# Weight sums of the up-projection made during the mixers' projection, a third activation fetched early in the down stage, the delayed norm's fetches pinned

## The chip, the cores and the metric

The kernel runs on one core of a Trainium2 chip. The metric is the device time of one execution in microseconds; the figure for a kernel is the median of its runs. All numbers below are microseconds (us) unless marked ns. The engines are PE (TensorE, matmuls), PEld (its weight loads), DVE (VectorE), ACT (ScalarE), POOL (GpSimd) and SP (SyncE, which here only issues DMAs). L12 is line 12 of the kernel before, unless a line of the changed kernel is named as such.

## The reference

One layer of a trunk is computed for 2048 prompt rows and 8 x 16 sample rows of width 1024, all in float32:

```
h = RMSNorm(x);  z = h @ w_in                      (1024 -> 3592)
A = chunk-band attention(z);  B = mLSTM(z)
x = x + RMSNorm(concat(A, B) @ w_out)              (1024 -> 1024)
u = RMSNorm(x) @ w_up                              (1024 -> 2 x 2816)
y = causal depthwise convolution of width 3 over u, plus bias
x = x + RMSNorm((gelu(y_gate) * y_up) @ w_down)    (2816 -> 1024)
```

The outputs are x, the new key and value caches, the mLSTM states and the last two rows of u for the next convolution.

## The kernel before

**Precision.** Every float32 operand of a matmul is split into a high part (a cast on ACT, L1250) and a low part (raw minus high, a subtraction on DVE, L1251), and each product is three matmuls (`mm3`, L93 to L97). So each block of weights costs a load, a cast and a subtraction before PE can use it.

**The mixers' projection** (L1186 to L1241) runs in two halves of the rows, and in each half over 14 groups of columns of w_in (`GROUPS`, L1140). A group's weights are loaded in two pieces of 512 KB by `load_group` (L1144 to L1165, tile wi_raw, issue at L1155, cast at L1161, subtraction at L1162) while the group before is on PE. The work of a group is cut into units; after each unit the loop steps the weights of the next group, the norms of the next half's rows (`norm_steps`), and `pump` (L171), which mixes in pieces of attention and mLSTM according to their costs on PE and DVE. Almost all loads of this stage stand in the one queue of SP, in order: weights (wi_raw), keys and values (kraw, qraw, vraw, and the caches skr, svr), masks and biases, states. A load whose buffer is still in use holds what stands behind it. The row of a norm's gains is read by `norm_row` (L87) into a tile with the tag "grow", of which there is one buffer. Then `project` (L956) multiplies with w_out, adds the residual on POOL (L1021) and stores it.

**The FFN** runs in three blocks of rows (6, 6 and 5 tiles of 128 rows). Each block has an up stage and a down stage.

*Up stage* (L1462 to L1501). For each of the 22 f (128 gate columns and 128 up columns) the two 128-column products of the two halves of the block are made with seven block products in place of eight, in the manner of Strassen and Winograd; each is 12 matmuls, so 84 per f. Four of the seven weight blocks are sums of blocks of w_up. The quarters of a raw [128, 2048] slice w_up[f] are called a11, a12, a22, a21. In block 0, `load_quads` (L1255) loads the four raw quarters, makes four sums on POOL (L1267, 128x512 each) and stores them to a DRAM scratch `wsd` (L1269); blocks 1 and 2 load three raw quarters and four sums from `wsd` (L1278). `load_up` (L1282) splits the seven quarters. `ahead_of` calls it two half steps ahead. Behind the products come the corrections on DVE (L1475, L1477, L1490, L1403), the convolution `conv` (copies of a two-row halo on POOL L1414 and L1419, ACT L1422, DVE L1423 and L1424, the Gelu on ACT L1426), the product g on DVE (L1496, and L1499 for the sample rows), and its store to DRAM gd (L1501).

*Down stage* (L1507 to L1580). For each half dh of the output columns and each k of 22, g of f=k is fetched again (`fetch`, L1438 to L1447, tile gr), split (`split_g`, L1449, tiles gh and gl) and multiplied, 18 matmuls of 128x512 per k (15 in block 2). k=0 and k=1 of dh=0 are fetched in the up stage, at f=20, and split at f=21; after that `fetch(dh, k + 1)` follows the split of k. gr of k=2 stands in SP's queue behind the store of g of f=21.

*The delayed norm.* For blocks 0 and 1 the last norm of a row tile needs sums that are ready only at the end of the block. `later` (L1353 to L1365) does it in pieces, each two fetches (L1357, L1358), a product on DVE (L1360), an add on POOL (L1361) and a store (L1362). The pieces are handed out in the next block's down stage between the k.

**What sets the order.** The program is written in one order, and a scheduler (the tile context at L1675) moves each instruction on its engine by a time that it works out itself when the kernel is built; `keep_in_program_order` exempts an instruction from that. So an operation can end up far ahead of the place where it is written. Buffers also bind: tiles q (`quad`, L1041) have 11 buffers, tiles yq (`row`, L1044) three.

Of the kernel before, what the change touches and what calls it, by code (L numbers as in the profile page):

```python
# [17 lines left out]
P = 128  # L18
# [26 lines left out]
def hymba_step(ctx: ExitStack, tc: tile.TileContext, I: dict, O: dict):  # L45
# [1085 lines left out]
    def late_B():  # L1131

        for i in (P5, P2, P4, P3):
# [3 lines left out]
            nc.scalar.copy(hi, lo.bitcast(F32))  # L1137
            nc.vector.tensor_tensor(lo, lo.bitcast(F32), hi, op=ALU.subtract)  # L1138

    GROUPS = ["va0", "qk0", "qk1", "va1", "qk2", "qk3", "qb0", "vo0", "qb1", "vo1", "qb2", "vo2", "qb3", "vo3"]  # L1140
    SRC = {g: i for i, g in enumerate(["va0", "qk0", "qk1", "va1", "qk2", "qk3",
                                       "qb0", "vo0", "qb1", "vo1", "qb2", "vo2", "qb3", "vo3"])}
# [24 lines left out]
    def norm_steps(half):  # L1167

        for ci, tiles in enumerate(HALVES[half]):
            ch = phT.tile([P, 2, KT, 384], F32R, tag="hT", name=f"hT{half}_{ci}", bufs=3)  # L1170
            chunks.append(ch)
            for j, t in enumerate(tiles):
                norm_tile(t, ch, j, ps_big)
                yield 0.9, 2.5
# [3 lines left out]
    pipes += [Pipe(att_stream()), Pipe(mem_stream())]  # L1178
    chunks = []
    norms = norm_steps(0)  # L1180
    next(norms)
    pend = load_group(0)
    for _ in pend[2]:
# [2 lines left out]
    for n_, (half, gi) in enumerate(seq):  # L1186
        wh, wl, _ = pend
        split = iter([])
        if n_ + 1 < len(seq):
            pend = load_group(seq[n_ + 1][1])  # L1190
            split = pend[2]
        g = GROUPS[gi]
        i = int(g[2])
        nm = f"{g}_{half}"
        if g[:2] == "va":
            it = group_rows(wh, wl, half, chunks, vd[i], nm, 264 if gi == 0 else 256,
                            [O["v_prompt"][i], O["v_sample"][i].unsqueeze(1)])
        elif g[:2] == "qk":
            it = group_T(wh, wl, half, chunks, [qTd[i], kTd[i]], [-(DA ** -0.5), None], nm,
                         [None, [O["k_prompt"][i], O["k_sample"][i]]])  # L1200
        elif g[:2] == "qb":
            it = group_T(wh, wl, half, chunks, [[t_[:, c, :] for t_ in qkbd[i]] for c in range(2)],
                         [None, DH ** -0.5], nm)
        else:
            it = group_rows(wh, wl, half, chunks, vobd[i], nm)
        if half == 0 and gi == 13:
            chunks = []
            norms = norm_steps(1)
        if n_ == len(seq) - 1:
            out = project([0, 1, 2, 3, 4, 5, 6, 7, SAMPLE, 8, 9, 10, 11, 12, 13, 14, 15])  # L1210
            split = w_out_steps()
            next(split)
            next(out)
        for u, (pe, dve) in enumerate(it):
            ahead = []
            if n_ < len(seq) - 1 or u >= 6:
                ahead.append(next(split, (0.0, 0.0)))
            if n_ == len(seq) - 1 and u == 12:
                ahead.append(next(out))
            if (half == 0 and gi == 13 and u >= 6 and u % 2 == 0) or (gi == 0 and u % 2 == 0):  # L1220
                ahead.append(next(norms, (0.0, 0.0)))
            pump(pe + sum(a[0] for a in ahead), dve + sum(a[1] for a in ahead))
        for _ in split:
            pass
        if gi == 0:
            if half == 0:
                nc.sync.dma_start(bgate, I["b_gate"].broadcast_to([P, 8]))
                nc.sync.dma_start(gatt, I["g_att"])
                heads.append(build_bias)
                mems.append(lambda: prep(prep_sample()))  # L1230
            mems.append(lambda half=half: prep(prep_prompt(half)))
        if g[:2] == "qk":
            attention(i, half)
            if half == 0 and i == 3:
                heads.insert(len(heads) % 4, lambda: attention_sample(0, EARLY))
            if half == 1 and i == 0:
                heads.insert(len(heads) % 4, lambda: attention_sample(EARLY, DB))
        if g[:2] == "vo":
            mems.append(lambda i=i, half=half: mlstm(i, half))
            if half == 0:  # L1240
                mems.append(lambda i=i: mlstm_sample(i))  # L1241
# [8 lines left out]
        nc.scalar.copy(h, r)  # L1250
        nc.vector.tensor_tensor(l, r, h, op=ALU.subtract)  # L1251

    raws = {}

    def load_quads(b, f, g):  # L1255

        src = lambda i: I["w_up"][f][:, i * 512:(i + 1) * 512]
        if b == 0 and g == 0:
            q = []
            for i in range(4):  # L1260
                q.append(quad(f"wu{f}_{i}"))
                nc.sync.dma_start(q[i], src(i))
            a11, a12, a22, a21 = q
            s1, s2, s3, s4 = [quad(f"ws{f}_{i}") for i in range(4)]
            for o, x, y, op in ((s1, a21, a22, ALU.add), (s2, s1, a11, ALU.subtract), (s3, a11, a21, ALU.subtract),
                                (s4, a12, s2, ALU.subtract)):
                nc.gpsimd.tensor_tensor(o, x, y, op=op)  # L1267
            for i, o in enumerate((s2, s3, s1, s4)):
                nc.sync.dma_start(wsd[f][:, i * 512:(i + 1) * 512], o)  # L1269
            raws[f] = [a12, a22, s4]  # L1270
            return [a11, s2, s3, s1]
        if b == 0:
            return raws.pop(f)
        kept = lambda i: wsd[f][:, i * 512:(i + 1) * 512]
        out = []
        for i, s_ in enumerate([[src(0), kept(0), kept(1), kept(2)], [src(1), src(2), kept(3)]][g]):
            r = quad(f"wu{b}_{f}_{g}_{i}")
            nc.sync.dma_start(r, s_)  # L1278
            out.append(r)
        return out  # L1280
# [72 lines left out]
    def later(t, rs):  # L1353

        def unit(half):
            v, x, c = quad(f"f{half}{t}"), quad(f"x{half}{t}"), half * 512
            nc.sync.dma_start(v, (f0d, f1d)[half][t])  # L1357
            nc.sync.dma_start(x, x2d[t][:, c:c + 512])  # L1358
            yield 0.0, 0.0
            nc.vector.scalar_tensor_tensor(v, v, rs, g3[:, c:c + 512], op0=ALU.mult, op1=ALU.mult)  # L1360
            nc.gpsimd.tensor_tensor(v, v, x, op=ALU.add)  # L1361
            nc.sync.dma_start(out_rows(t)[:, c:c + 512], v)  # L1362
            yield 0.0, 1.0

        return [unit(half) for half in range(2)]  # L1365
# [21 lines left out]
    for b, tiles in enumerate(FBLOCKS):  # L1387
# [48 lines left out]
        n2 = nt * P // 2  # L1436

        def fetch(dh, k, early=False):  # L1438
            if k >= NF:
                return  # L1440
            if early:
                g[dh, k] = [quad(f"gr{b}_{dh}_{k}_{i}")[:, :n2] for i in range(2)]
                for i, r in enumerate(g[dh, k]):
                    nc.sync.dma_start(r, gd[b][k][:, i * n2:(i + 1) * n2])
            else:
                g[dh, k] = row(f"gr{b}_{dh}_{k}")
                nc.sync.dma_start(g[dh, k][:, :2 * n2], gd[b][k][:, :2 * n2])  # L1447
# [14 lines left out]
        for f in range(NF):  # L1462
# [20 lines left out]
            if f == NF - 1:  # L1483
                split_g(0, 0, w3_tile)
                split_g(0, 1, w3_tile)
            ug = u_tile(f"ug{nm}")
            product(P2, w[0], a, onto=True)
            nc.scalar.copy(ug[:, 2:2 + n], a[:, :n])
# [18 lines left out]
        for dh in range(2):  # L1507
# [9 lines left out]
            for c in range(6):  # L1517
# [16 lines left out]
                if tail and c >= 4:  # L1534
                    places = []
                    for i in ((0, 1) if c == 4 else (2,)):
                        t_ = p3.tile([P, 2, 4, 384], F32R, tag=f"B{i}", name=f"gtail{i}", bufs=1)
                        t_ = t_.rearrange("p a k n -> p (a k n)")
                        places += [t_[:, x * 768:(x + 1) * 768] for x in range(4)]
                    for k in ks:  # L1540
                        split_g(dh, k, lambda name: places.pop())
                        fetch(dh, k + 1)
                    if c == 4:
                        wh4, wl4 = wh, wl
                        continue
                    for j in range(nt):
                        for k in range(16, 20):
                            down(j, k, wh4, wl4)
                        for k in ks:
                            down(j, k, wh, wl)  # L1550
                        finish(b, j, load_rest(b, j), *evacuate(b, j, accs[j], 1), res[j])
                    continue
                for k in ks:
                    if (dh, k) not in parts:
                        split_g(dh, k, w3_tile)
                    if k + 1 == NF and dh == 0:
                        fetch(1, 0)
                    elif dh == 1 or k >= 1:
                        fetch(dh, k + 1)
                    for j in order if k == NF - 1 else range(nt):  # L1560
                        down(j, k, wh, wl)
                    if k >= 1:
                        ahead.step()
# [115 lines left out]
```

## Time and profile before

| what | value |
|---|---|
| median of 3 runs | 2866.95 us (2863.55 to 2875.75) |
| profiled execution, its own time | 2872.21 us |
| span of its trace | 2870.5 us |
| TensorE clock granted (mean) | 0.985 |
| up stage of block 0, of block 1 | about 1331 to 1694, 1894 to 2219 |
| last up product of block 2 | 2698 |
| loads of w_up (256 KB each) / of the sums / stores of sums | 220 / 176 / 88 |

The profile lists, for one execution, the busy time of each engine, groups of equal instructions with their mean duration and the idle time of the engine ahead of them, with what ended that idle time (the sign <-). A row of the timeline is: start, duration, engine, line, operation, output <- inputs, shapes, and in square brackets the idle time before it and its releaser. A row of the view by windows gives busy time and instruction count of each engine in a stretch, then the granted clock, the busy share of the DMA engines and GB/s.

### The profile page before, as it was taken

To read this page: it belongs to the slowest core of one execution; us is meant where nothing else is said; L and a number is where in the kernel's file an instruction comes from. 1 tells how busy PE (TensorE), PEld (TensorE's weight loads), DVE (VectorE), ACT (ScalarE), POOL (GpSimd) and SP (SyncE) were. 2 spreads that over 40 slices of the span, in tenths; PEclk is the share of its full clock that TensorE was granted. 3 is DMA by queue.
4 is the path that set the end of the run, shared out by engine and by line. 5 is a ranking of instruction groups with operands and counts; after the bars stand their busy time and mean duration, and the time that the engine had idled before them with its cause. 6 is when DMAs were issued, how large, how long until landed. Compare 5 with 4: busy or idle time off the path is not lost.

```text
span 2870.5 us, 47064 instructions
## 1 busy us (share of the span) xinstructions
PE 2752.3 (96%) x16587; PEld 2566.0 (89%) x16587; DVE 1899.5 (66%) x3345; ACT 1405.6 (49%) x2827; POOL 561.8 (20%) x964
## 2 busy tenths in 40 slices
PE   8899999999999999999999989999999899999898
PEld 7899989989899998878989978899999778999787
DVE  5344455645456678576999976467777754888755
ACT  4344555534356676343444445345554443555433
POOL 1000010211000003255555410011111210222311
PEclk9999999999999999999999999999999999999899
DMA  4544355556555564366444545645444775555766
GB/s 163 171 120 124 110 174 152 177 161 194 169 154 153 157 192 148 106 198 211 152 166 144 167 141 171 217 147 158 148 149 162 235 242 160 171 174 181 234 222 200
DMA packets 312122, 486.04 MB, mean 169 GB/s; under 512 B 55282, under 2 KB 148174, under 8 KB 311758
## 3 DMA queue, kind: packets, MB, share of 16 engines
q1 hardware_dynamic: 273294, 449.21, 50.1%
q10 hardware_dynamic: 38592, 33.83, 3.5%
q8 instruction: 130, 2.13, 0.3%
q14 instruction: 106, 0.87, 0.1%
HBM read 359.36 MB, written 126.70 MB: 169 GB/s over the span
## 4 chain that ended last, share of the span: by engine, by line
PE 49%; DVE 7%; issue 2%; DMA 2%; ACT 1%; POOL 1%; SPq 0%; DVEq 0%; ACTq 0%; POOLq 0%
PE uec L95 5%; PE uec L96 5%; PE uec L97 5%; PE dn L97 4%; PE dn L96 4%; PE dn L95 4%; PE ua L95 3%; PE ua L97 2%; PE ua L96 2%; PE dnm L95 2%; PE dnm L97 2%; PE dnm L96 2%; PE wo L97 2%; PE wo L95 2%; PE wo L96 2%
## 5 line engine op out<-in xcount | busy, mean ns | idle before, releaser
L95 PE MATMUL uec<-B,wuh 128*128 128x384 f32 (+1 forms) x720 | 236.2, 329 | 7.9 <-DVE uu L1490 7.9
L1251 DVE TENSOR_TENSOR gl<-gr,gh 128x768 fp32r<-128x768 f32 (+3 forms) x132 | 117.8, 897 | 188.2 <-ACT gh L1250 188.1
L96 PE MATMUL uec<-B,wuh 128*128 128x384 f32 (+1 forms) x720 | 235.6, 327 | 0.4 <-DVE B L1138 0.4
L97 PE MATMUL uec<-B,wul 128*128 128x384 f32 (+1 forms) x720 | 233.0, 327 | 0.0
L1250 ACT CAST gh<-gr 128x768 fp32r<-128x768 f32 (+3 forms) x132 | 101.5, 773 | 238.2 <-PE dn L96 200.0
L95 PE MATMUL dn<-wdh,gh 128*128 128x512 f32 x466 | 185.1, 397 | 7.9 <-DVE ug L1403 7.9
L96 PE MATMUL dn<-wdl,gh 128*128 128x512 f32 x466 | 185.9, 399 | 0.0
L1251 DVE TENSOR_TENSOR wul<-wu,wuh 128x512 fp32r<-128x512 f32 x255 | 179.3, 742 | 9.4 <-ACT wuh L1250 6.6
L1250 ACT CAST wuh<-wu 128x512 fp32r<-128x512 f32 x255 | 141.6, 617 | 71.3 <-PE uec L96 67.5
L97 PE MATMUL dn<-wdh,gl 128*128 128x512 f32 x466 | 170.4, 398 | 0.0
L96 PE MATMUL vo<-wi_l,hT 128*128 128x256 f32 x544 | 155.7, 286 | 0.0
L95 PE MATMUL vo<-wi_h,hT 128*128 128x256 f32 x544 | 154.9, 285 | 0.6 <-DVE mt L199 0.6
L97 PE MATMUL vo<-wi_h,hT 128*128 128x256 f32 x544 | 155.3, 285 | 0.0
L387 DVE CUSTOM_DVE_ANT_0 tmp<-s,nb 128x640 f32<-128x640 f32 (+4 forms) x128 | 94.3, 737 | 77.1 <-PE s L377 73.6
L95 PEld LDWEIGHTS uec<-B,wuh 128*128 128x128 f32 x720 | 135.4, 188 | 11.0 <-DVE uu L1490 9.8
L96 PEld LDWEIGHTS uec<-B,wuh 128*128 128x128 f32 x720 | 135.5, 188 | 0.9 <-DVE B L1138 0.7
L97 PEld LDWEIGHTS uec<-B,wul 128*128 128x128 f32 x720 | 135.1, 188 | 0.0
L95 PE MATMUL qk<-hT,wi_h 128*128 128x384 f32 (+1 forms) x384 | 128.8, 335 | 4.2 <-ACT qk_st L226 3.6
L95 PE MATMUL dnm<-wdh,gh 128*128 128x512 f32 x252 | 101.8, 407 | 31.6 <-ACT gh L1250 29.8
L388 ACT ACTIVATE tmp<-tmp,mn 128x640 f32<-128x640 f32 (+4 forms) x128 | 97.6, 762 | 70.2 <-DVE mn L387 65.9
L400 DVE TENSOR_TENSOR ptl<-pt,pth 128x640 fp32r<-128x640 f32 (+4 forms) x128 | 93.5, 737 | 55.8 <-ACT pth L399 54.7
L97 PE MATMUL qk<-hT,wi_l 128*128 128x384 f32 (+1 forms) x384 | 128.9, 336 | 0.0
(409 smaller groups left out, 9065.4 us busy)
## 6 DMA issues: line engine op xcount, KB each, us to landing
wu<-in_w_up SPq DMA_DIRECT2D x220, 256.0 KB, 3.8
wu<-wsd SPq DMA_DIRECT2D x176, 256.0 KB, 5.0
wdr<-in_w_down SPq DMA_DIRECT2D x132, 256.0 KB, 4.5
gr<-gd SPq DMA_DIRECT2D x84, 384.0 KB, 3.5
wi_raw<-in_w_in SPq DMA_DIRECT2D x52, 512.0 KB, 4.4
wsd<-ws SPq DMA_DIRECT2D x88, 256.0 KB, 3.2
gd<-g SPq DMA_DIRECT2D x44, 384.0 KB, 2.8
kraw<-kTd SPq DMA_DIRECT2D x112, 128.0 KB, 3.4
```

The lines of the kernel that those rows point to most:

```text
L95: nc.tensor.matmul(out, ah, bh, start=start, stop=False, skip_group_check=onto)
L96: nc.tensor.matmul(out, ah, bl, start=False, stop=False, skip_group_check=onto)
L97: nc.tensor.matmul(out, al, bh, start=False, stop=stop, skip_group_check=onto)
L387: nc.vector.tensor_tensor_reduce(o_, s_, b_, 1.0, 3e38, ALU.add, ALU.min, accum_out=mn)
L388: nc.scalar.activation(tmp[:, :n], tmp[:, :n], AF.Exp, bias=mn, scale=-1.0, accum_out=rsum[:, i % 4, hh:hh + 1])
L400: nc.vector.tensor_tensor(s.ptl[:, sl, qc], ptv, s.pth[:, sl, qc], op=ALU.subtract)
L1250: nc.scalar.copy(h, r)
L1251: nc.vector.tensor_tensor(l, r, h, op=ALU.subtract)
```

## The change

Three things are done.

1. A generator `sum_steps` makes the sums of all 22 f in the projection. An item is half of an f (256 of 512 columns of the four quarters): one load of 512 KB into a tile of the tag "grow" (one buffer), two empty steps, four POOL operations of 128x256 in place, two empty steps, one store of 512 KB to `wsd[f]`, two empty steps. The loop steps it once per unit for the groups 2 to 12 of each half: 156 units in the first half, which are 26 items, the other 18 in the second half. Since the gains of the first norm are in the same single buffer, `g0.clear()` makes the second half read them again. `load_quads` now reads three raw quarters and four sums in every block, block 0 included (154 loads in block 0 in place of 88 loads and 88 stores).
2. g of k=2 for the down stage is fetched at f=21, and from there each fetch is two k ahead, across the change of dh too.
3. The two fetches of a piece of the delayed norm keep their place in program order.

```
+    def sum_steps():
+        for f in range(NF):
+            for e in range(2):
+                view = lambda t: t.rearrange("p (q c) -> p q c", q=4)[:, :, e * 256:(e + 1) * 256]
+                w = const.tile([P, 4, 256], F32, tag="grow", name=f"ws{f}_{e}")
+                nc.sync.dma_start(w, view(I["w_up"][f]))
+                yield
+                yield
+                a11, a12, a22, a21 = [w[:, i] for i in range(4)]
+                nc.gpsimd.tensor_tensor(a22, a21, a22, op=ALU.add)
+                nc.gpsimd.tensor_tensor(a21, a11, a21, op=ALU.subtract)
+                nc.gpsimd.tensor_tensor(a11, a22, a11, op=ALU.subtract)
+                nc.gpsimd.tensor_tensor(a12, a12, a11, op=ALU.subtract)
+                yield
+                yield
+                nc.sync.dma_start(view(wsd[f]), w)
+                yield
+                yield
...
+    sums = sum_steps()
...
         if half == 0 and gi == 13:
             chunks = []
             norms = norm_steps(1)
+            g0.clear()
...
+            if 2 <= gi < 13:
+                next(sums, None)
             pump(pe + sum(a[0] for a in ahead), dve + sum(a[1] for a in ahead))
...
     def load_quads(b, f, g):
-        src = lambda i: I["w_up"][f][:, i * 512:(i + 1) * 512]
-        if b == 0 and g == 0:
...
-            for o, x, y, op in ((s1, a21, a22, ALU.add), (s2, s1, a11, ALU.subtract), (s3, a11, a21, ALU.subtract),
-                                (s4, a12, s2, ALU.subtract)):
-                nc.gpsimd.tensor_tensor(o, x, y, op=op)
-            for i, o in enumerate((s2, s3, s1, s4)):
-                nc.sync.dma_start(wsd[f][:, i * 512:(i + 1) * 512], o)
...
+        own = lambda i: I["w_up"][f][:, i * 512:(i + 1) * 512]
         kept = lambda i: wsd[f][:, i * 512:(i + 1) * 512]
         out = []
-        for i, s_ in enumerate([[src(0), kept(0), kept(1), kept(2)], [src(1), src(2), kept(3)]][g]):
+        for i, s_ in enumerate([[own(0), kept(0), kept(3), kept(2)], [own(1), own(2), kept(1)]][g]):
...
-            nc.sync.dma_start(v, (f0d, f1d)[half][t])
-            nc.sync.dma_start(x, x2d[t][:, c:c + 512])
+            tc.keep_in_program_order(nc.sync.dma_start(v, (f0d, f1d)[half][t]))
+            tc.keep_in_program_order(nc.sync.dma_start(x, x2d[t][:, c:c + 512]))
...
         def fetch(dh, k, early=False):
-            if k >= NF:
+            if dh > 1 or k >= NF:
                 return
...
             if f == NF - 1:
                 split_g(0, 0, w3_tile)
                 split_g(0, 1, w3_tile)
+                fetch(0, 2, True)
...
                     for k in ks:
                         split_g(dh, k, lambda name: places.pop())
-                        fetch(dh, k + 1)
+                        fetch(dh, k + 2)
...
-                    if k + 1 == NF and dh == 0:
-                        fetch(1, 0)
-                    elif dh == 1 or k >= 1:
-                        fetch(dh, k + 1)
+                    if dh == 1 or k >= 1:
+                        fetch(dh + (k + 2) // NF, (k + 2) % NF)
```

More of the change, by code (lines that the diff above doesn't have):

```diff
@@ L1251, in split @@
         nc.vector.tensor_tensor(l, r, h, op=ALU.subtract)
-    raws = {}
     def load_quads(b, f, g):
-        src = lambda i: I["w_up"][f][:, i * 512:(i + 1) * 512]
-        if b == 0 and g == 0:
[L1259 to L1264, printed above, removed]
-            for o, x, y, op in ((s1, a21, a22, ALU.add), (s2, s1, a11, ALU.subtract), (s3, a11, a21, ALU.subtract),
-                                (s4, a12, s2, ALU.subtract)):
-                nc.gpsimd.tensor_tensor(o, x, y, op=op)
-            for i, o in enumerate((s2, s3, s1, s4)):
-                nc.sync.dma_start(wsd[f][:, i * 512:(i + 1) * 512], o)
[L1270 to L1273, printed above, removed]
+        own = lambda i: I["w_up"][f][:, i * 512:(i + 1) * 512]
         kept = lambda i: wsd[f][:, i * 512:(i + 1) * 512]
         out = []
-        for i, s_ in enumerate([[src(0), kept(0), kept(1), kept(2)], [src(1), src(2), kept(3)]][g]):
+        for i, s_ in enumerate([[own(0), kept(0), kept(3), kept(2)], [own(1), own(2), kept(1)]][g]):
             r = quad(f"wu{b}_{f}_{g}_{i}")
```

## The prediction

> **What bounds the kernel now.** I read the page's engine line first, then the windows by stage, then, inside the stages that the change touches, the waits, the groups by shape and the timeline.
>
> ```profile
> PE 2752.3 (96%) x16587; PEld 2566.0 (89%) x16587; DVE 1899.5 (66%) x3345; ACT 1405.6 (49%) x2827; POOL 561.8 (20%) x964
> ```
> ```profile
> core 0: us, PE busy (x) PEld busy (x) DVE busy (x) ACT busy (x) POOL busy (x), PEclk, DMA share, GB/s
> 60.00:960.00 900.00, 874.53 (x6203) 849.77 (x6202) 472.00 (x1175) 447.66 (x1079) 73.34 (x228) 0.99 0.52 154
> ...
> 1340.00:1670.00 330.00, 308.30 (x1700) 298.67 (x1699) 305.98 (x347) 151.46 (x244) 172.63 (x161) 0.98 0.49 159
> 1890.00:2200.00 310.00, 310.00 (x1780) 309.96 (x1779) 240.35 (x357) 158.76 (x263) 42.58 (x94) 1.00 0.50 156
> ```
>
> PE is busy 96% of the span, so the average says "bound by TensorE". The stages differ. In the up stage of block 1 (1890 to 2200) PE has no gap at all: 1780 matmuls in 310 us, 0.174 us each. In the up stage of block 0 (1340 to 1670), which does the same products, it gets 1700 matmuls into 330 us, 0.194 us each, while DVE is busy 306 of 330 and POOL 173. That stage is bound by DVE, and the projection (60 to 960) by PE, with 25.5 us of idle PE in 900.
>
> ```profile
> 1402.66 0.85 ACT L1426 ACTIVATE y<-y 128x768 f32<-128x768 f32 x1 [3.93 <-DVE y L1424]
> ...
> 1686.14 0.85 ACT L1426 ACTIVATE y<-y 128x768 f32<-128x768 f32 x1 [0.37 <-DVE y L1424]
> ...
> 1951.49 0.85 ACT L1426 ACTIVATE y<-y 128x768 f32<-128x768 f32 x1 [1.64 <-DVE y L1424]
> ...
> 2210.98 0.85 ACT L1426 ACTIVATE y<-y 128x768 f32<-128x768 f32 x1 [0.74 <-DVE y L1424]
> ```
>
> The Gelu runs once per f. The four rows are f=2 and f=20 of block 0 and of block 1: 283.48 us for 18 f (15.75 each) against 259.49 (14.42 each). **One f costs 1.33 us more in block 0.** Who is longer there:
>
> ```profile
> L1267 POOL TENSOR_TENSOR ws<-wu,wu 128x512 f32<-128x512 f32 x40 | 64.1, 1603 | 60.0 <-DMA wu<-in_w_up 48.8 <-DVE wul L1251 7.6 <-DVE x L1477 3.2
> ```
> ```profile
> L1251 DVE TENSOR_TENSOR wul<-ws,wuh 128x512 fp32r<-128x512 f32 x44 | 49.5, 1145 | 0.0
> ...
> L1403 DVE TENSOR_TENSOR ug<-x,uec 128x384 f32<-128x384 f32 x16 | 8.7, 546 | 3.9 <-PE uec L97 3.9
> ```
> ```profile
> L1251 DVE TENSOR_TENSOR wul<-wu,wuh 128x512 fp32r<-128x512 f32 x81 | 52.1, 684 | 0.0
> ...
> L1403 DVE TENSOR_TENSOR ug<-x,uec 128x384 f32<-128x384 f32 x17 | 9.4, 555 | 28.7 <-PE uec L97 28.7
> ```
> ```profile
> PE ua L95 <- ACT wuh L1250: 9.4, 7, 1.9
> ```
>
> The first fence is POOL's sums in block 0, the second DVE beside them, the third the same DVE operations in block 1 without sums. A subtraction of two SBUF operands takes 1145 ns beside POOL and 684 alone; an add with one operand in PSUM takes 546 and 555. The last row is what PE feels of it: weights that arrive late. And a late arrival costs more than its wait:
>
> ```profile
> 1459.55 0.47 PE L95 MATMUL ua<-B,wuh 128*128 128x384 f32 x1 [1.86 <-ACT wuh L1250]
> ...
> 1462.80 0.52 PE L97 MATMUL ua<-B,wul 128*128 128x384 f32 x1
> 1463.12 0.40 PE L95 MATMUL ua<-B,wuh 128*128 128x384 f32 x1
> 1463.36 0.34 PE L96 MATMUL ua<-B,wuh 128*128 128x384 f32 x1
> 1463.53 0.34 PE L97 MATMUL ua<-B,wul 128*128 128x384 f32 x1
> ```
>
> After a gap of 1.86 us matmuls start 0.32 us apart instead of 0.17 for about 3.5 us: about 1.6 us on top of the wait.
>
> **The change, part by part.** The sum is made against the profiled execution, 2872.21 us (span 2870.5), 0.2% above the median of 2866.95; I scale at the end.
>
> *A. Sums gone from block 0.* Each f loses four POOL operations of 128x512 and four stores; its seven quarters are then loaded as in block 1. What is late next is known from block 1: nothing, PE at 310 of 310. So 21 steps of f by 1.33 us: **−28**. Bounds: −20 if a third of the difference has another cause, −36 if the first two f, which start late behind the same sums, gain some 4 us each beside that.
>
> *B. The starts of the three down stages.* The last up product ends, its u goes through conv, Gelu and the product g, is stored to gd, and the queue of SP fetches gr of k=2 only behind that store. PE meanwhile has k=0 and k=1 and then stands.
>
> ```profile
> 1693.82 0.34 PE L97 MATMUL uec<-B,wul 128*128 128x384 f32 x1
> ...
> 1695.15 0.39 PE L96 MATMUL dn<-wdl,gh 128*128 128x512 f32 x1
> ...
> 1695.38 0.40 PE L97 MATMUL dn<-wdh,gl 128*128 128x512 f32 x1
> ...
> 1708.18 0.80 PE L95 MATMUL dnm<-wdh,gh 128*128 128x512 f32 x1 [10.32 <-ACT gh L1250]
> ```
> ```profile
> 2218.43 0.34 PE L97 MATMUL uec<-B,wul 128*128 128x384 f32 x1
> ...
> 2220.78 0.75 DVE L1360 SCALAR_TENSOR_TENSOR f<-f,drs,norm_row 128x512 f32<-128x512 f32 x1 [3.85 <-DMA f<-f1d]
> ...
> 2237.14 0.80 PE L95 MATMUL dnm<-wdh,gh 128*128 128x512 f32 x1 [8.90 <-ACT gh L1250]
> ```
> ```profile
> 2698.20 0.30 PE L97 MATMUL uec<-B,wul 128*128 128x320 f32 x1
> ...
> 2714.45 0.80 PE L95 MATMUL dnm<-wdh,gh 128*128 128x512 f32 x1 [10.59 <-ACT gh L1250]
> ```
>
> From the last up product to the restart: 14.0, 18.4 and 16.0 us. With the change k=2 is fetched at f=21, so its 18 matmuls (15 in block 2), 0.23 us apart, fill 4.1 us (3.5) of the gap; what is late next is k=3, whose fetch still stands behind the same store. Against it: the split of k=2 puts two half subtractions of about 0.5 us between the two conv steps of the last f on DVE, +1.0. So −3 in block 0. In block 1 the delayed norm's DVE step (the L1360 row), which waits 3.85 us for its own fetch with the last ug queued behind it, stands after g of f=21 in the new order (the order of the changed kernel's instructions on each engine, which its scheduler fixes when it is built), because its fetch is pinned into the down stage: the 18.4 becomes 14.0, another −4.4, so −7.5. In block 2 the norm's steps leave the same stretch, 16.0 towards 13.5: −2.5, so about −5. Together **−16**; bounds −8 (only the pinned part, and one microsecond more) and −20 (the half rate after each gap goes too). The pinned fetches themselves go beside down products, where SP is not waited for.
>
> *C. Sums in the projection.* 44 items, one after another through one buffer: a 512 KB load, four POOL operations of 128x256, a 512 KB store. 26 lie in the first half, 18 in the second. One more load of a norm row changes nothing that PE waits for.
>
> ```profile
> wi_raw<-in_w_in SPq DMA_DIRECT2D x52, 512.0 KB, 4.4
> ```
> ```profile
> x2d<-mx SPq DMA_DIRECT2D x17, 512.0 KB, 2.9
> ```
> ```profile
> L1361 POOL TENSOR_TENSOR f<-f,x x24: 1257/1625/2887, 2211.4 to 2745.3; 128x512 f32<-128x512 f32 x24
> ```
> ```profile
> SPq L1155 <- DVE wi_l L1162: 71.8, 27, 11.0
> ```
> ```profile
> 57.85 7.71 SPq L1155 DMA_DIRECT2D wi_raw<-in_w_in  x2
> ...
> 331.74 0.37 SPq L1155 DMA_DIRECT2D wi_raw<-in_w_in  x1
> ...
> 368.79 0.34 PE L95 MATMUL qb<-hT,wi_h 128*128 128x384 f32 x1
> ```
> ```profile
> PE cus L775 <- DMA cs<-in_state_c: 4.7, 4, 1.8
> ```
>
> No row shows a 128x256 sum; half of the shortest 128x512 add (1257 ns) is 0.63, half of the contended 1603 is 0.80. I take 0.65, being nearest to the uncontended add, as DVE is at half load here. An item is then 4.4 + 4x0.65 + 2.9 + 0.7 for two issues = **10.6 us** (10.5 to 11.2 by the two ends). The queue of SP is in order, so it stands at each store until POOL is done and at each load until the store before has landed, about 10 us per item, and the weight and attention loads stand behind. In the new order the first item comes right behind the load at 57.85 and the 26th ahead of the one at 331.74. 57.85 + 26x10.6 = 333: the chain just keeps up. If it lags, the weights have 368.79 − 331.74 = 37 us, less 4.4 of landing and about 3 of splitting: 30 us of slack. POOL's own work behind these waits is small (73 of 900 us). SP already stands 71.8 us for weight buffers, which shows that it runs ahead.
>
> Cost: not below nothing, since nothing leaves this stage. Above: when the chain lags past the slack (rival 1), 40. I take **+10**: one item in five makes PE wait as long as the cus row's mean (4.7/4 = 1.2 us), 9 x 1.2.
>
> DVE pays too: the trace shows two-SBUF subtractions held by POOL. The Trainium skill, SBUF — State Buffer, section "Who interferes with whom", says that a DVE instruction with two SBUF inputs contends with a GpSimd instruction reading SBUF, and one with a single SBUF input does not; the rows 1145 against 684 and 546 against 555 agree. By that rule moving the sums only moves the contention, at most DVE's excess of block 0; with that falling on PE as it does in block 0 the sum would be −6 in place of −34. I don't take that, since DVE is idle 428 of 900 us here against 24 of 330 there.
>
> Sum: −28 − 16 + 10 = **−34**, 2838.2 on the profiled execution, times 2866.95/2872.21 = **2833.0**.
>
> **The rivals.**
>
> 1. *The sum chain paces the queue.* If an item takes 13 us instead of 10.6 (a slower load beside 150 GB/s of other traffic, or the four operations at 0.8 and SP held elsewhere between), the 26th is done at 57.85 + 338 = 396, 64 us late, 34 past the slack. Net −34 + 34 = 0, **2867**. It begins at 11.7 us per item. For it: one buffer, three transfers of hand-over per item and SP's order fixed. Against: the new order leaves about 10.5 us per item, near the rows. Chance 0.19, most of it within 0.5%.
>
> 2. *Every item of the first half stops PE (slower).* The mechanism is the half rate after a short gap: behind each store in SP's queue stands a load that PE needs, PE waits 1.0 us and then pays the 1.6 above. 26 x 2.6 = 68 instead of 10: net +24, **2891**. It turns to a loss from (28+16)/2.6 = 17 items. For it: the 1.86 us gap already brought the slow stretch. Against: between 143 and 359 us PE waits hardly at all today, and weights come 30 us early. Chance 0.09. The Trainium skill, TensorE: Matmul & The Clock Gate, section "Why this matters for your kernels", puts the limit at gaps of about 3 us; by it such waits would cost 26 us alone and the change would still win (−18, 2849). The row of a slow stretch after 1.86 us speaks against that limit here.
>
> 3. *The early third fetch does nothing*: PE waits for k=3 as late, and the delay of g eats the rest. Then B is −6 and the sum −24, **2843**. For it: the fetch of k=3 is still behind the last store. Chance 0.10.
>
> 4. *Block 0 has another bound*, so that A is near nothing: −6, **2861**. Against: block 1 runs the same loads and products at full PE. Chance 0.04.
>
> **How the numbers follow.** Forecast 0.58, rivals 0.19, 0.09, 0.10, 0.04. The forecast's own range is 2815 to 2850 (A −36 and B −20 with C 0 would be 2811; A −20, B −8, C +10 is 2849). About 0.5%, 14 us, is what a measurement of this kernel can tell: faster means under 2852.6. Faster: 0.58 + 0.10 + 0.05 of rival 1, **0.73**. Same: 0.13 of rival 1, 0.04 of rival 4 and the mild end of rival 2: **0.18**. Slower: **0.09**. The range of 8 in 10 leaves out rival 2 and the upper part of rival 1: **2812 to 2867**.
>
> **What would show it.** A is right if Gelus of block 0 are 14.4 apart, the subtractions 684 ns, and PE waits for no wuh. B is right if PE's waits for gh after the last up product fall to about 7 us, end at k=3, and no L1360 step lies ahead of the last g. C is right if the interval from one sum load to the next is near 10.6 us and PE's idle time between 60 and 960 grows from 25 to about 35; rival 1 shows as weight loads landing after their group should start near 370 us, rival 2 as idle time beyond 60 with many restarts at half rate. The forecast fails most easily in the item's 10.6 us, which no row of this trace has measured as a whole.

## The result, and the profile after

The changed kernel takes 2907.70 us (median of 4 runs, 2903.86 to 2915.54), the kernel before 2869.47 (4 runs). The ratio is 1.0136, 95% interval 1.0103 to 1.0170: slower by 38 us, where 34 us faster was forecast. The profiled execution, 2915.54 us with a span of 2913.8, is the slowest of the four; its span is 43.3 longer than before's.

First the engine line of the page, and the view by windows: the projection, then the up stages of block 0 and block 1, shifted to where they now lie.

```profile
PE 2770.1 (95%) x16587; PEld 2586.5 (89%) x16587; DVE 1839.7 (63%) x3348; ACT 1406.7 (48%) x2830; POOL 553.9 (19%) x1052
```
```profile
core 0: us, PE busy (x) PEld busy (x) DVE busy (x) ACT busy (x) POOL busy (x), PEclk, DMA share, GB/s
60.00:960.00 900.00, 814.44 (x5469) 782.41 (x5468) 428.54 (x1029) 386.03 (x927) 195.48 (x378) 0.95 0.63 189
1425.00:1735.00 310.00, 308.79 (x1772) 308.46 (x1771) 246.24 (x359) 162.41 (x256) 41.06 (x85) 1.00 0.53 168
1950.00:2260.00 310.00, 310.00 (x1781) 310.00 (x1780) 239.97 (x356) 156.44 (x257) 41.27 (x92) 1.00 0.49 154
```

Block 0's up stage now looks like block 1's: PE full, DVE from 306 of 330 us down to 246 of 310. The loss is all in the first row. PE gets 5469 matmuls into the 900 us in place of 6203. Its idle time went from 25.5 to 85.6 us, and the granted clock from 0.99 to 0.95.

In the timeline, the Gelu of f=2 and f=20 of block 0:

```profile
1482.39 0.84 ACT L1432 ACTIVATE y<-y 128x768 f32<-128x768 f32 x1
...
1743.62 0.85 ACT L1432 ACTIVATE y<-y 128x768 f32<-128x768 f32 x1 [0.37 <-DVE y L1430]
```

That is 261.23 us for 18 f, 14.51 each. Between fixed marks of the two traces the 43 us divide as follows. The lag is the delay of the same matmul of the projection against before (both have 4752 of them).

| stretch | before | after | difference |
|---|---|---|---|
| start to the last matmul of the projection | 1055.5 | 1147.7 | +92.2 |
| from there to the first Gelu of block 0 | 316.2 | 307.0 | −9.2 |
| first Gelu to that of f=20, block 0 | 314.4 | 288.9 | −25.5 |
| from there to the end | 1184.4 | 1170.2 | −14.2 |

The lag grows in steps while items run and hardly at all between: 25.5 us at the matmul that before starts at 226.0, 44.7 at 293.6, 54.1 at 349.6 (the first half's items have ended), 56.4 at 514.9, 66.7 at 659.8, 92.7 from 816.3 on. On average that is 2.1 us for each of the 44 items, about the same in both halves.

Why, in SP's queue (timeline of SP, 209 to 229 us) and POOL's:

```profile
209.14 0.58 SPq L1146 DMA_DIRECT2D ws<-in_w_up  x1
217.09 0.57 SPq L1156 DMA_DIRECT2D wsd<-ws  x1
220.38 0.55 SPq L1146 DMA_DIRECT2D ws<-in_w_up  x1
221.02 0.57 SPq L1175 DMA_DIRECT2D wi_raw<-in_w_in  x1
221.69 0.56 SPq L434 DMA_DIRECT2D mixd<-attst  x1
227.31 0.55 SPq L1156 DMA_DIRECT2D wsd<-ws  x1
228.47 0.33 SPq L1175 DMA_DIRECT2D wi_raw<-in_w_in  x1
```
```profile
213.89 0.73 POOL L1150 TENSOR_TENSOR ws<-ws 128x256 f32<-128x256 f32 x1 [8.39 <-DMA ws<-in_w_up]
214.71 0.73 POOL L1151 TENSOR_TENSOR ws<-ws 128x256 f32<-128x256 f32 x1
215.52 0.73 POOL L1152 TENSOR_TENSOR ws<-ws 128x256 f32<-128x256 f32 x1
216.33 0.73 POOL L1153 TENSOR_TENSOR ws<-ws 128x256 f32<-128x256 f32 x1
```

From 209.7 to 220.4 SP issues nothing but the store of the sums: it stands 7.4 us for load and adds, then 2.7 us for the store before the next load may use the buffer. The weight load of 221.02 stands behind both. What it does to PE shows in the timelines of ACT and PE:

```profile
226.07 0.62 ACT L1181 CAST wi_h<-wi_raw 128x512 fp32r<-128x512 f32 x1 [9.34 <-DMA wi_raw<-in_w_in]
...
227.12 0.36 ACT L399 CAST pth<-pt 128x256 fp32r<-128x256 f32 x1
```
```profile
227.53 0.58 PE L412 MATMUL ot<-pth,vhl 128*128 128x256 f32 x1 [5.63 <-ACT pth L399]
```

ACT works in order too. It stands 9.34 us at the cast of the late weights, and behind that cast stands a cast of attention (pth) that PE needs at once. PE then waits 5.63 us, and the lag goes from 17.0 to 23.0. The gap of 7.7 us at 302 has the same chain (ACT stood 10.68 us at the weights), and so has that of 5.4 us at 258, there with a late load of values (vraw, 9.74 us). The view of waits sums this up, for SP, then ACT (the profile before, then the changed kernel), then PE, 60 to 960:

```profile
SPq L1156 <- POOL ws L1153: 82.4, 29, 5.2
SPq L1146 <- DMA wsd<-ws: 79.8, 34, 4.6
...
SPq L1156 <- DMA ws<-in_w_up: 30.4, 14, 4.1
```
```profile
ACT wi_h L1161 <- DMA wi_raw<-in_w_in: 30.3, 19, 4.1
```
```profile
ACT wi_h L1181 <- DMA wi_raw<-in_w_in: 80.0, 19, 11.6
```
```profile
PE ot L412 <- ACT pth L399: 16.0, 4, 5.6
PE pt L67 <- ACT tmp L388: 10.8, 5, 6.2
PE vo L95 <- ACT vo_st L224: 9.0, 2, 7.7
```

SP stands 193 us for the sums alone. ACT waits 80 us for weights (30 before) and does nothing else meanwhile; PE then waits for attention pieces and evacuations (copies out of PSUM) that have nothing to do with the sums (of the three rows of PE, before has the second alone, with 2.3 us). Many of these gaps also cost afterwards:

```profile
310.23 0.58 PE L95 MATMUL vo<-wi_h,hT 128*128 128x256 f32 x1 [7.73 <-ACT vo_st L224]
310.61 0.42 PE L96 MATMUL vo<-wi_l,hT 128*128 128x256 f32 x1
...
314.88 0.41 PE L413 MATMUL ot<-ptl,vhl 128*128 128x256 f32 x1
315.09 0.33 PE L412 MATMUL ot<-pth,vhl 128*128 128x256 f32 x1
315.27 0.28 PE L413 MATMUL ot<-ptl,vhl 128*128 128x256 f32 x1
```

For 4.9 us the matmuls start 0.21 us apart; the granted clock there is 0.50. At a granted clock of 1.00 it is 0.11 to 0.12, as in the last two of the projection:

```profile
1147.60 0.28 PE L96 MATMUL vo<-wi_l,hT 128*128 128x256 f32 x1
1147.71 0.28 PE L97 MATMUL vo<-wi_h,hT 128*128 128x256 f32 x1
```

The two parts add up: 60 us more idle time and, by the rounded clocks, (0.99 − 0.95) x 900 = 36 us of clock, 96 against a lag of 92.

### The profile page after: what moved, and what is told of

Read it like the earlier page. It is cut to its first block, busy times and chain, and to the rows that moved or that the text cites. A ratio compares the mean times of both kernels' runs of the same rounds, so it can differ in the third digit from the quotient of the medians.

```text
span 2913.8 us, 47323 instructions
## 1 busy us (share of the span) xinstructions
PE 2770.1 (95%) x16587; PEld 2586.5 (89%) x16587; DVE 1839.7 (63%) x3348; ACT 1406.7 (48%) x2830; POOL 553.9 (19%) x1052
## 4 chain that ended last, share of the span: by engine, by line
PE 54%; DMA 2%; DVE 2%; ACT 1%; issue 1%; POOL 1%; SPq 0%; DVEq 0%; POOLq 0%; ACTq 0%
PE uec L95 6%; PE uec L96 6%; PE uec L97 6%; PE dn L96 3%; PE dn L95 3%; PE dn L97 3%; PE ua L97 3%; PE ua L96 3%; PE ua L95 3%; PE dnm L95 2%; PE dnm L97 2%; PE dnm L96 2%; PE wo L95 2%; PE wo L96 2%; PE wo L97 2%; PE ub L96 1%
## 5 line engine op out<-in xcount | busy, mean ns | idle before, releaser
L1274 ACT CAST wuh<-wu 128x512 fp32r<-128x512 f32 x315 | 173.0, 617 | 78.7 <-PE uec L96 74.9
L1275 DVE TENSOR_TENSOR wul<-wu,wuh 128x512 fp32r<-128x512 f32 x315 | 202.1, 685 | 2.8 <-DMA x2d<-mx 2.8
L95 PE MATMUL qk<-hT,wi_h 128*128 128x384 f32 (+1 forms) x384 | 133.3, 347 | 0.7 <-DVE gates L273 0.7
L96 PE MATMUL qk<-hT,wi_h 128*128 128x384 f32 (+1 forms) x384 | 132.4, 345 | 0.0
L1274 ACT CAST wu<-wu 128x512 fp32r<-128x512 f32 x147 | 84.7, 617 | 98.2 <-PE uec L96 64.0
L1182 DVE TENSOR_TENSOR wi_l<-wi_raw,wi_h 128x512 fp32r<-128x512 f32 (+1 forms) x112 | 78.4, 730 | 84.2 <-ACT wi_h L1181 81.8
```

The lines of the kernel that those rows point to most:

```text
L95: nc.tensor.matmul(out, ah, bh, start=start, stop=False, skip_group_check=onto)
L96: nc.tensor.matmul(out, ah, bl, start=False, stop=False, skip_group_check=onto)
L1182: nc.vector.tensor_tensor(l[:, c], r, h[:, c], op=ALU.subtract)
```

## The experiments

Theory 1: SP's in-order queue stands at each store and load of a sum, and the loads behind it come late. Theory 2: the added bytes slow the other loads. Theory 3: POOL's adds, through POOL's own order or DVE, are what costs. "Before" in these runs lay at 2865.5 to 2869.1. Where a kernel has a single run, its lag is uncertain by some 10 us or more: the changed kernel and E2 have the same order of instructions in the projection, and their profiled executions lag 92 and 71. The lag is always that of the profiled execution, which for the changed kernel lies 8 us above its median, for E3 6 below and for E5 10 below; where kernels have several runs, the medians compare them better.

**E1, the down-stage edits alone.** The kernel before with `fetch(0, 2, True)`, fetches two k ahead, and the two pinned fetches; no sums.

> The kernel before with the two down-stage edits alone (third activation fetched early, the delayed norm's fetches pinned), no sums in the projection. Between the Gelu marks the changed kernel gained 1.7 us from block 0 to block 1, 5.5 from block 1 to block 2, 2 in block 2's up stage and 5 after it, 14 in all. All theories: 14 us faster than before, about 2855, with the projection and block 0's up stage as before. If these gains hang on the sums being gone from block 0, nearer to 2863.

2850.43 (5 runs), ratio 0.9943 (0.9931 to 0.9956): 17 us faster than before and ahead of both kernels. The waits of PE for gh, in the three down starts:

```profile
1703.42 0.80 PE L95 MATMUL dnm<-wdh,gh 128*128 128x512 f32 x1 [7.00 <-ACT gh L1250]
...
2223.62 0.79 PE L95 MATMUL dnm<-wdh,gh 128*128 128x512 f32 x1 [5.39 <-ACT gh L1250]
...
2696.35 0.66 PE L95 MATMUL dnm<-wdh,gh 128*128 128x512 f32 x1 [4.59 <-ACT gh L1250]
```

10.3, 8.9 and 10.6 became 7.0, 5.4 and 4.6, and the wait for ug in block 1 fell from 4.2 to 0.65.

**E2, the sums alone.** The changed kernel with those two edits undone.

> The changed kernel with the two down-stage edits undone: the sums alone. All theories: the projection 92 us late as in the changed kernel, block 0's up stage 25 us shorter, the end of the projection stage some 10 shorter, so about 57 above before, 2925.

2905.69 (one run). Block 0's Gelus are as in the changed kernel (288.9 us from f=0 to f=20). The lag is 71 in place of 92, so the run came out 20 below the expectation, with the same instructions in the same order: the lag itself scatters.

**E3, the sums' DMAs on POOL's queue.**

```
-                nc.sync.dma_start(w, view(I["w_up"][f]))
+                nc.gpsimd.dma_start(w, view(I["w_up"][f]))
...
-                nc.sync.dma_start(view(wsd[f]), w)
+                nc.gpsimd.dma_start(view(wsd[f]), w)
```

> The changed kernel with the sums' 44 loads and 44 stores issued by POOL in place of SP; traffic, POOL's adds and the one buffer stay. Theory 1 (SP's in-order queue stands at each store and each load of a sum, and everything behind it is late): SP is free, the lag of the projection falls from 92 us to under 25, time 2820 to 2845. Theory 2 (the 45 MB of added traffic slow the other loads): lag as before, about 2905. Theory 3 (POOL's own order: its adds and, now, its DMA issues stand ahead of masks and gates): lag as before or more, 2905 to 2930.

2895.23 (4 runs), ratio 1.0098 (1.0083 to 1.0114). At the matmul of 293.6 the lag is 9 us in place of 45, as theory 1 wants; then it jumps by some 29 us in one place and ends at 66. Without the jump some 37 would remain, still above the 25 that theory 1 allowed. The place, in the timelines of PE and SP:

```profile
409.38 0.59 PE L95 MATMUL ss<-skh,zhl 128*128 128x264 f32 x1 [28.78 <-ACT skh L846]
```
```profile
403.37 0.33 SPq L89 DMA_DIRECT2D norm_row<-in_norm_g  x1
403.80 0.54 SPq L839 DMA_DIRECT2D own<-kTs  x1
```

The second reading of the norm row waits in SP's queue for the last sum's store, since it uses the same buffer; the sample keys (own) stand behind it. "One more load changes nothing that PE waits for" was wrong.

**E4, the same bytes without a wait.** Each item is one DMA from the weights into the scratch; no buffer, no adds. The sums are left out: the scratch holds raw quarters.

> The changed kernel, but each item is one DMA from the weights straight into the scratch: the same 22 MB read and written at the same places, no buffer, no adds, nothing to wait for (the sums are left out: the scratch holds raw quarters). Theory 1 and theory 3: lag under 15 us, about 2825. Theory 2: lag of 60 to 90, 2880 to 2905.

2879.19 (one run), lag 55. It tells less than was hoped: having nothing to wait for, all 44 copies were moved to the start by the scheduler. The lag of 63 was there by the 170th matmul, and none was added afterwards. As a measure it says that the bytes alone cost some 60 us when they come at one go, ahead of the first work.

**E5, the norm row's second reading on POOL's queue too.** E3 with `(q or nc.sync).dma_start(...)` in `norm_row`, POOL's queue for the second reading.

> The sums' DMAs on POOL's queue as before, and now the second reading of the norm row, which has to wait for the last sum's store because it shares the one buffer, also on POOL's queue. In the last run this read stood at the head of SP's queue from about 377 to 403 us and PE then had one gap of 28.8 us. Theory 1 (what stands in SP's queue sets the lag): that gap goes, the lag at the end of the projection falls from 66 to 35 or less, time about 2860. Theory 2 (added traffic): the gap comes back elsewhere, 2890 to 2900.

2886.27 (4 runs), ratio 1.0063 (1.0042 to 1.0085). It missed: a gap of 24.4 us stays at the same place, but now for another reason. Timelines of PE and POOL:

```profile
401.72 0.59 PE L95 MATMUL ss<-skh,zhl 128*128 128x264 f32 x1 [24.43 <-ACT skh L846]
```
```profile
396.62 0.75 POOL L1156 DMA_DIRECT2D wsd<-ws  x1 [0.30 <-POOL ws L1153]
400.25 0.56 POOL L89 DMA_DIRECT2D norm_row<-in_norm_g  x1 [2.88 <-DMA wsd<-ws]
400.79 0.47 POOL L842 COPY skr<-own 128x16 f32<-128x16 f32 x3
```

The copies of the sample keys (L842) stand in POOL's own order behind the last sums. So POOL's own order counts (theory 3), though by the waits in it and not by the adds: here too the chain of sums holds the in-order queue that it is put into.

**E6, the same bytes, each copy kept in program order.** E4 with `tc.keep_in_program_order` around the copy.

> The last kernel with direct copies let the scheduler move all 44 copies to the start, and the whole lag of 63 us arose there ahead of the first unit. Here each copy keeps its place in program order, so 46 MB are spread over the projection and nothing waits for them (the sums are left out: the scratch holds raw quarters). Theory 1: lag under 15, about 2825. Theory 2: lag of 50 or more spread over the stage, 2870 to 2905.

2851.05 (one run). The windows row of the projection:

```profile
60.00:960.00 900.00, 857.69 (x6013) 830.56 (x6012) 455.83 (x1143) 430.76 (x1044) 70.07 (x224) 0.98 0.59 176
```

With nearly the traffic of the changed kernel (176 against 189 GB/s) PE is idle 42 us, not 86, and the lag is 22: more than theory 1 allowed, far less than theory 2.

**E7, 17 f, nine units per item in place of six,** on SP's queue; the last 5 f are summed in block 0 as before.

> The changed kernel with nine units between items in place of six, which leaves room for 17 of the 22 f; the last 5 f are summed in block 0 as before. SP's queue as in the changed kernel. The traffic of the projection is 77%, the time per item about 16 to 20 us against a chain of 13. Theory 1: SP no longer stands for long, the lag falls well below 77% of 92, to 30 or less: time about 2850 to 2860. Theory 2 (proportional to traffic): lag 71, time about 2893.

2874.77 (6 runs), ratio 1.0030 (1.0018 to 1.0043). Lag 49, 1.4 us per item in place of 2.1. A third of the cost per item went, not most of it. Loads still follow each other by 13.3 us; only more units pass meanwhile.

**E8, the same with POOL's queue as in E5.**

> Both: 17 f nine units apart, their DMAs and the norm row's second reading on POOL's queue. Theory 1: lag 15 to 25, the lowest of these, time about 2835 to 2845, below the down-stage edits alone at 2850. Theory 2: about 2890.

2859.69 (10 runs), ratio 0.9976 (0.9964 to 0.9988): faster than before, but 9 behind E1. Lag 29, 0.84 per item, and the gaps of E3 and E5 are gone. With 17 f, block 0 gains 15 us over E1 from f=2 to f=20, 3 at its start and 7 ahead of it; that doesn't pay for the lag, 31 against E1.

**E9, the four adds left out.** Load, store, buffer and queue stay; the scratch gets raw quarters.

> The changed kernel on SP's queue, with the four adds of each item left out (the scratch gets raw quarters). Load, store, buffer, queue and traffic stay; the time from a load's landing to the store shrinks by the 3.3 us that four adds of 0.74 us and their hand-overs took. Theory 1: SP stands some 9 us per item in place of 13, the lag at the end of the projection falls from 92 to 40 to 60, time about 2860 to 2880. Theory 3 (POOL's adds, by the shared port or POOL's own order, are what costs): lag near the 22 of the traffic alone, time about 2840.

2897.12 (one run), lag 74. It missed both: POOL's adds are not the cost (theory 3), and a shorter chain doesn't help. Items now follow each other by 9.9 us in place of 13.4, but the new build has fewer other DMAs between a load and its store (2.4 in place of 4.7 on average), so SP still stands 105 us for the loads to land and 73 for the stores, 178 in place of 193.

**E10 and E11, the two down-stage edits apart.**

> The kernel before with only the third activation fetched early. By the prediction's terms: 3 in block 0, 3 in block 1 (its product still behind the delayed norm's step), 2.5 in block 2: about 2859. If PE then waits as long for k=3, 2866.

> The kernel before with only the delayed norm's two fetches pinned. By the prediction's terms: nothing in block 0, 4.4 in block 1, 2.5 in block 2: about 2860. Both edits together gave 17, so if they don't hang on each other, this one and the other add up to that.

2861.24 (11 runs), ratio 0.9984 (0.9975 to 0.9993), and 2862.02 (11 runs), ratio 0.9991 (0.9983 to 1.0000). Apart they give some 3 to 4 each, together 17. Block 2 shows why, the wait for gh with the third fetch alone and with the pin alone:

```profile
2710.47 0.80 PE L95 MATMUL dnm<-wdh,gh 128*128 128x512 f32 x1 [10.27 <-ACT gh L1250]
```
```profile
2704.09 0.80 PE L95 MATMUL dnm<-wdh,gh 128*128 128x512 f32 x1 [8.65 <-ACT gh L1250]
```

10.3 and 8.7, but 4.6 with both (E1): k=2 shortens the wait only where the last g isn't itself late, and with the third fetch alone a step of the norm (L1360 at 2701.10, with 2.33 us of idle DVE before it) stands right ahead of it. Summed over the three starts, PE's waits for gh, gl and ug are 37.8 us before, 30.4 with the third alone, 31.8 with the pin alone and 20.1 with both.

**E12, 7 f in the first half on POOL's queue,** 14 items in groups 4 to 12, with the down-stage edits.

> Both down-stage edits, and sums of the first 7 f alone, 14 items nine units apart in groups 4 to 12 of the first half, their DMAs on POOL's queue; the other 15 f are summed in block 0 as before. In the run with 17 f so placed the first half's lag grew by about 5 us after its first items, 0.4 per item, against 0.67 per item gained in block 0. Theory 1: lag 5 to 8, gain 7 x 1.3 plus 3 at the start of block 0, so 2843 to 2848, ahead of the down-stage edits alone at 2850. Theory 2 (half a microsecond per item of traffic and up): no better than 2850.

2875.85 (7 runs), ratio 1.0037 (1.0022 to 1.0052). A miss. The projection ended on before's time (lag 0.1), but that doesn't price the items, since this build moved work of attention and mLSTM out of it (49 matmuls of it more than in E1 stand behind the projection). Between the projection and block 0 it lost 20 us against E1 (335.9 in place of 315.9): PE there waits more for DVE, in the view of waits from 1050 to 1400 (E1 has 3.0 and 1.6 us in these rows):

```profile
PE mT_pt L67 <- DVE mr L979: 10.3, 6, 4.6
PE h2T_pt L1081 <- DVE x2r L1073: 7.3, 2, 6.0
```

These two rows make 13 of the 20 us. Why this build chose another order was not found.

**E13, the chain without the bytes.** The changed kernel with 8 of 256 columns moved per item, sixteen small adds in place of four (4.5 us together in place of 3.3), every block loading raw quarters (the sums are left out).

> The changed kernel, but each item's load and store move 8 of 256 columns, and its four adds of 128x256 are sixteen of 128x8, about as long together; queue, buffer, order of waits stay (the sums are left out: every block loads raw quarters). An item still has a load's latency, the adds and a store's latency one after another, some 7 to 10 us in place of 13. Theory 1 (standing in the queue is enough): lag 40 to 60. If standing only costs together with the traffic (loads that come late because they are also slower): lag under 20.

2900.18 (one run), lag 70. SP's waits:

```profile
SPq L1157 <- POOL ws L1154: 92.1, 27, 5.2
SPq L1146 <- DMA wsd<-ws: 43.3, 33, 2.2
```

This is the run that decides. Nearly without the sums' traffic, at 145 GB/s (before: 154), the lag is 70, above even the expected 40 to 60 and as large as E2's 71 with all the bytes. Take away the bytes (E13) or the adds (E9, lag 74), and a lag of 70 or more remains: neither is what costs. What these runs share is the chain's standing in SP's queue. How much the bytes add is not shown: 70 and E6's 22 make the changed kernel's 92, but not E2's 71. Over the five runs with the chain in SP's queue the lag goes with SP's standing: 193 us and 92, 187 and 71 (E2), 178 and 74 (E9), 156 and 70 (E13), 130 and 49 (E7), a ratio of 0.37 to 0.48.

**E14 and E15, 8 f and 6 f in the first half on POOL's queue,** nine and twelve units apart in groups 2 to 12.

> Down-stage edits, and 8 f as 16 items nine units apart in groups 2 to 12 of the first half, DMAs on POOL's queue. If the 7 f lost only by the order that its build gave the stage after the projection: about 2845. If the cost of items is bound to be what they gain: 2850 to 2860.

> The same with 6 f as 12 items twelve units apart. By the same two readings: about 2846, or 2850 to 2856.

2878.88 (8 runs), ratio 1.0033 (1.0020 to 1.0045), and 2881.20 (5 runs), ratio 1.0036 (1.0022 to 1.0050). Both missed, with lags of only 6 and 12 but the same loss of 20 us ahead of block 0 as in E12 (337.4 and 335.9). None of the numbers of f that were tried, 6 to 22, beats leaving the sums where they were (E1).

## Why the prediction was wrong

**A, −28 for the sums gone from block 0: right.** The step per f fell from 15.75 to 14.51 (forecast 14.42), and PE no longer waits there. From the first Gelu to f=20 it gave 25.5 us; another 9.2 came ahead of it, where only the bound had counted something. Together 35, at the bound of 36. The runs fit the mechanism as told: wul fell from 1145 to 685 ns, and E2 shows the same gain without the other edits. The stores of the sums left block 0 together with the adds, so no run separates the two.

**B, −16 for the down starts: right.** The same stretches gave 14 us in the changed kernel and 16 in E1 (17 by the medians). By block, the changed kernel gained 1.7, 5.5 and 5 where −3, −7.5 and −5 stood in the sum, and another 2 in block 2's up stage, which the sum did not have. PE's waits for gh fell to 7.0, 7.0 and 4.5. What I did not see is that the two edits need each other.

**C, +10 for the sums in the projection: the step that failed.** It measured +92, nine times as much, and turns −34 into +38. Its range allowed for 40 at most, in rival 1. Three things in it were wrong; the second is the one that counts.

- *The item.* 10.6 us was too short: load 4.6 (4.4 assumed), adds 0.74 each and 0.82 apart (0.65), store 3.6 (2.9), issues 0.56 (0.35), 12.6 in sum, and 13.4 from load to load. But this isn't the cause: in E9 the items followed each other by 9.9 us and the lag was still 74.
- *The slack.* I set the chain's end against one late weight load near 370 us and allowed 30 us before PE feels anything. The lag was 25 us by 226. The 30 us were counted from the load to PE's first use of the weights. But ACT casts them ahead of that (before, the load of 331.74 at 336.21, while PE used it at 368.79), in its own order, and stands there when they are late; casts and evacuations that PE needs at once stand behind. Keys and values of attention, behind the sums in the same queue, have no such slack either (the gap at 258). I had "the weight and attention loads stand behind" in the text and reckoned with PE's use of the weights alone. The hint was in the profile before: ACT already waited 30.3 us for weights, so for ACT they didn't come 30 us early.
- *The price of a stall.* I took one item in five at 1.2 us. An item cost 2.1 us on average, of which by the clock some 0.8 is the slow stretch behind the gaps. It isn't the same for every item: from 60 to 960 PE has 42 gaps over 0.3 us (19 before), and the 11 over 3 us (2 before) make 50 of the 86 us.

**The rivals.** Rival 1 (the chain paces the queue, 2867) had the right place and the wrong law: it expected nothing until the chain lags by 30 us, and a shorter item as the cure; E9 and E13 speak against both. Rival 2 (each item stops PE and a slow stretch follows, 2891, chance 0.09) came nearest: loads late behind the sums stop PE, and a slow stretch follows. Its law, 1.0 us at each item, isn't what the trace shows (few long gaps, by way of ACT, in both halves), and that 44 x 2.1 = 92 lies near its 26 x 2.6 = 68 is in part luck. I had held it down because PE hardly waited between 143 and 359 us before; that a stage has no waits now says nothing of the loads' margin. Rivals 3 and 4 are out by E1 and E2; with the third fetch alone, rival 3 would have held in block 2 (E10).

**Contention and short gaps.** The Trainium skill, SBUF — State Buffer, section "Who interferes with whom", says that a DVE instruction with two SBUF inputs contends with a GpSimd instruction that reads SBUF. Moving the sums so made a loss possible that I gave no weight. The trace agrees, and the loss is small: beside the moved adds wi_l rose from 690 to 740 ns, and without them (E9) it was 691 with a lag of 74. The slow stretches bear on the limit of about 3 us for idle gaps that the Trainium skill, TensorE: Matmul & The Clock Gate, section "Why this matters for your kernels", gives. The changed kernel's trace, like the row of 1.86 us in the profile before, speaks against it as a limit: after a gap of 1.90 us (to 485.03) and one of 2.34 us (to 694.38) the granted clock was 0.50 for some 3.4 us, while after one of 1.91 us (to 387.29) it stayed at 1.00.

**What is left open.** Why the lag scatters between 71 and 92 for one order of instructions; how far theory 2's 22 us would overlap with the standing in one kernel, since E6, E9 and E13 are single runs, each with an order of its own; and the 20 us ahead of block 0 in E12, E14 and E15. A second buffer for the sums was not run, so whether it would shorten SP's standing isn't shown.

## What to carry to other kernels

Before work is moved into a stage "where an engine is idle", look at the queue that its transfers share: a load, compute, store chain through one buffer makes an in-order queue stand twice per item (here 193 us in 900), and what stands behind pays, however idle the engines are. Price such an item by what stands behind it, not by the chain's own length, and count the slow matmuls after the gaps. Count the slack of a load to the first engine that takes it in order, not to the last one that uses it. And split a bundle of edits early: here two small edits worth 17 us lay hidden in a bundle that lost 38.

## What the runs showed of the hardware that was not expected

A 512 KB load or store cut into runs of 1 KB took SP 0.56 us to issue at the median; a weight load of the same size (wi_raw) took 0.34 before and 0.37 after, single ones up to 0.6. A POOL add of 128x256 takes 0.74 us and its successor starts 0.82 after it, more than half of the shortest 128x512 add (1.26 us). 23 MB copied within DRAM (46 MB read and written) put PE back by 63 us when they came at one go (E4), and by 22 when spread over the stage (E6).
